# Attention heads with v stationary: probabilities scaled, turned by key block, output feature-major

## The chip, the cores and the metric

One core of one Trainium2 chip runs the whole program in one launch. TensorE (PE in the profile; PEld are its weight loads) multiplies, VectorE (DVE) and ScalarE (ACT) do elementwise work, GpSimd (POOL) a little of it, and SyncE's queue (SP) issues the transfers. The metric is the device time of one execution in microseconds; what is told of the kernel before is the median of its runs and one profiled execution.

## The reference

Three blocks follow one another on 512 tokens of 2048 features, all float32. Only the attention heads of the first and third block matter here.

```python
# block 1: 16 heads of 64, three dilated patterns mixed by their log-sum-exp
for window, dilation in ((128, 1), (512, 4), (2048, 16)):
    o, lse = dilated_pattern_attention(q, k, v, slopes, window, dilation)
weights = softmax(stack(lses), axis=0)
o = einsum('pbhs,pbhsd->bhsd', weights, stack(outs))
y_a = o * silu(g_a)

# block 3: 16 query heads on 4 key heads, blocks of 128, window 128, a sink per head
m = maximum(max(logits, axis=-1), sink)
p = exp(logits - m)
probs = p / (sum(p, axis=-1) + exp(sink - m))
out = einsum("bnhgqk,bnkhd->bnqhgd", probs, vb)
```

The kernel computes the first as one causal attention over 512 keys: the number of patterns that hold a key enters its bias as a logarithm, so that one softmax gives the mixture.

## The kernel before

Activations lie feature-major: 16 tiles of 128 features by 512 tokens. A **unit** is 128 output features of a projection: 16 feature tiles by 3 products (high and low halves of the split float32) into one PSUM bank of pool `pm`, 48 matmuls 128x512. They carry the names `pm<-a,wh` and `pm<-a,wl` and line L128 (the helper `mm`). A weight arrives by SP in pieces of 1024 columns; ScalarE makes its high half `wh` and VectorE its low half `wl`, into pools of five buffers each, ahead of the products.

Heads are generators. `drive` keeps 2 (block 1) or 5 (block 3) of them active; a head asks for a unit with `yield w, ct, h`, and each bare `yield` lets one step, 12 products of somebody's unit, be written in between. After every weight piece `bg` adds one step of background work: in blocks 1 and 2 the modulation products `ga<-gr` on VectorE (128x1024). A scheduler then sets the order on each engine from the dependencies; the four banks of pool `px` (tiles `x`) take everything that isn't a unit.

The dilated generator (`dilated`, eight pairs of heads in block 1, stretch 520 to 880 us) and the banded one (`swa`, eight pairs in block 3, mostly 2590 to 2960 us, one pair at a time) go alike. Per head and per block of 128 queries, scores of 128 to 512 keys are made (two matmuls), VectorE adds the bias and takes the extremum (L527, L1514), ScalarE exponentiates and sums (`den`). `turn` (L616) transposes the probabilities block by block of 128 keys with the identity `cst`, and ScalarE copies them out. `pv` then multiplies: the turned block 128x128 is stationary, 64 columns of v (`vt`, keys on partitions) move. The products of both heads lie in one bank with queries on the partitions; `finish_pair` divides by `den` on VectorE and transposes four blocks (L134, `tr4`) back to feature-major. `pipeline` writes scores, turn and product of neighbouring blocks one step apart, eight blocks for a dilated pair, four half-rows for a banded one.

The recurrence `hgrn` of block 1, which the prediction reads a row of, ends in a matmul `po[64 * r:64 * r + 64, c]` with a stationary of 64 columns: two chunks, one on each half of the output's partitions.

Of the kernel before, what the change touches and what calls it, by code (L numbers as in the profile page):

```python
# [14 lines left out]
AF = mybir.ActivationFunctionType  # L15
OP = mybir.AluOpType
AX = mybir.AxisListType.X

P = 128
T = 512  # L20
# [20 lines left out]
class Kernel:  # L41
# [524 lines left out]
    def dilated(self, p, h, w, ys):  # L566
        nc = self.nc
# [16 lines left out]
        self.act(vt, self.tr4(v))  # L584
        den = self.s(8)
        po = self.x()
        prs, pts = {}, {}

        def scores(i):
            qi, hh = i // 2, i % 2  # L590
            n = P * (qi + 1)
            sc = self.x()
            self.scores(sc[:, :n], q[hh][:, qi * P:(qi + 1) * P], [v[:, :n] for v in k[hh]])
            prs[i] = self.t()
            self.softmax_block(sc[:, :n], n, bts[hh][:, T - n:], den[:, i:i + 1], prs[i][:, :n])

        def turn(i):
            pts[i] = self.turn(prs.pop(i), i // 2 + 1)

        def out(i):  # L600
            qi, hh = i // 2, i % 2
            r = slice(64 * hh, 64 * hh + 64)
# [8 lines left out]

    def turn(self, pr, nb):

        b = self.x()
        for j in range(nb):
            self.nc.tensor.transpose(b[:, j * P:(j + 1) * P], pr[:, j * P:(j + 1) * P], self.ident)  # L616
        pt = self.t()
        self.act(pt[:, :nb * P], b[:, :nb * P])
# [8 lines left out]
    def finish_pair(self, po, den):  # L627

        rd = self.s(8)
        self.nc.vector.reciprocal(rd, den)  # L630
        on = self.t()
        self.tt(on.rearrange("p (n d) -> p n d", d=64), po.rearrange("p (n d) -> p n d", d=64),
                rd[:, :, None].to_broadcast([P, 8, 64]))
        yield
        ot = self.tr4(on)
        yo = self.y()
        self.act(yo, ot, scale=0.5)
        return yo

# [197 lines left out]
    def na(self, p, h, w, ys):  # L837
# [30 lines left out]
        yield  # L868
        vts = [self.turn(v, 4) for v in vs]
        den = self.s(8)  # L870
# [16 lines left out]
        def turn(j):  # L887
            pts[j] = self.turn(prs.pop(j), 4)

        def out(j):  # L890
            hh, half = j // 2, j % 2
            r = slice(64 * hh, 64 * hh + 64)
            pt = pts.pop(j)
            for i in range(2):
                cb = 2 * half + i
                self.pv(pt[:, 256 * i:256 * i + 256], vts[half], po[:, cb * P + 64 * hh:cb * P + 64 * hh + 64],
                        [(2 * i, r), (2 * i + 1, r)])

# [579 lines left out]
    def swa(self, i, h, w, kf, ys):  # L1478
# [18 lines left out]
        k, vt = kf[kv], self.vb[kv]  # L1497
        nm, den = self.s(8), self.s(8)
        po = self.x()
        prs, pts = {}, {}  # L1500

# [3 lines left out]

        def scores(j):
            hh, half = j // 2, j % 2
            hd = SWA_ORDER[2 * i + hh]
            sc, pr = self.x(), self.t()
            for qi, k0, c, n in blocks(half):  # L1510
                self.scores(sc[:, c:c + n], q[hh][:, qi * P:(qi + 1) * P], [a[:, k0 * P:k0 * P + n] for a in k[hh]])
            for qi, k0, c, n in blocks(half):
                m = nm[:, 2 * qi + hh:2 * qi + hh + 1]
                nc.vector.tensor_tensor_reduce(pr[:, c:c + n], sc[:, c:c + n], nbs[hh][:, 256 - n:256], 1.0,  # L1514
                                               self.nsink[:, hd:hd + 1], OP.add, OP.min, accum_out=m)
                self.act(pr[:, c:c + n], pr[:, c:c + n], AF.Exp, bias=m, scale=-1.0,
                         accum_out=den[:, 2 * qi + hh:2 * qi + hh + 1])
            prs[j] = pr

        def turn(j):  # L1520
            pts[j] = self.turn(prs.pop(j), 3 + j % 2)

        def out(j):
            hh, half = j // 2, j % 2
            r = slice(64 * hh, 64 * hh + 64)
            pt = pts.pop(j)
            for qi, k0, c, n in blocks(half):
                self.pv(pt[:, c:c + n], vt, po[:, qi * P + 64 * hh:qi * P + 64 * hh + 64],
                        [(k0 + b, r) for b in range(n // P)])

        yield from self.pipeline(4, scores, turn, out)
        es = self.s(8)
        for hh in range(2):
            hd = SWA_ORDER[2 * i + hh]
            self.act(es[:, hh::2], nm[:, hh::2], AF.Exp, bias=self.rowp[:, 16 + hd:17 + hd])
        self.tt(den, den, es, OP.add)
        ys[8 + i] = yield from self.finish_pair(po, den)

# [220 lines left out]
```

## Time and profile before

| | us |
|---|---|
| median of 3 runs (lowest, highest) | 3434.01 (3431.7, 3434.43) |
| profiled execution, its own time | 3428.47 |
| its span, first to last instruction | 3426.8 |
| TensorE busy | 3387.9 (99%) |
| VectorE busy | 1974.5 (58%) |
| ScalarE busy | 1277.3 (37%) |
| mean granted TensorE clock | 0.997 |

In a row of a group stand line, engine and operation, out<-in by the program's names, the shape (for matmuls ahead of it the stationary, partitions*columns), the number of instructions, then busy us, mean ns of one, and the idle time before them with what ended it. A row of the timeline begins with its start in us from the span's start and how long it was busy; like neighbours are merged (x8). A float32 matmul is two instructions, an fp32r one (units, scores) and a transposition are one.

### The profile page before, as it was taken

What the parts mean: (1) busy time and instruction counts of PE and PEld (TensorE: products, weight loads), DVE (VectorE), ACT (ScalarE), POOL (GpSimd) and SP (SyncE); (2) the same over time, 40 slices, a digit from 0 to 9 for tenths busy, and PEclk for the clock granted to TensorE, in tenths of its full rate; (3) what the DMA queues carried; (4) which work ended last, traced back from release to release, by engine and by line L of the source; (5) the groups of instructions that cost most, each with busy time, mean ns of one, the idle gap of its engine ahead of it and who ended that gap; (6) DMA issues with size and microseconds to landing.
All of it is one profiled execution on the core that took longest, in us unless ns stands there. A gap on an engine that the chain in (4) does not pass through costs nothing.

```text
span 3426.8 us, 44441 instructions
## 1 busy us (share of the span) xinstructions
PE 3387.9 (99%) x16688; PEld 2826.3 (82%) x16688; DVE 1974.5 (58%) x3593; ACT 1277.3 (37%) x2459; POOL 133.1 (4%) x156
## 2 busy tenths in 40 slices
PE   9999999999999999999999999999999999999999
PEld 7878888888888888888888888887888888888887
DVE  8677556556767555643367667666754333344552
ACT  4222244444334223544442243333334344432331
POOL 0000000000000000101100000000000000000000
PEclk9999999999999999999999999999999999999999
DMA  6355345435664445432234333322222233324442
GB/s 222 123 178 172 134 149 185 143 128 184 199 221 133 154 158 181 172 120 96 84 106 143 100 114 105 96 92 89 90 65 86 96 102 105 127 94 146 141 142 95
DMA packets 166168, 451.68 MB, mean 132 GB/s; under 512 B 26496, under 2 KB 47296, under 8 KB 165952
## 3 DMA queue, kind: packets, MB, share of 16 engines
q1 hardware_dynamic: 165952, 448.84, 39.8%
q8 instruction: 131, 2.15, 0.3%
q14 instruction: 85, 0.70, 0.1%
HBM read 423.58 MB, written 25.18 MB: 131 GB/s over the span
## 4 chain that ended last, share of the span: by engine, by line
PE 53%; DVE 4%; issue 1%; ACT 1%; POOL 0%; DMA 0%; SPq 0%; DVEq 0%; ACTq 0%; POOLq 0%
PE pm L128 46%; PE x L128 5%; DVE fp L117 1%; PE x L616 1%; PE x L134 1%; DVE wl L117 1%; DVE ft L1278 1%; DVE t L117 1%; DVE t L120 0%; ACT t L114 0%; POOL s L142 0%; ACT wh L114 0%; DVE s L1383 0%; DVE s L117 0%; DMA t<-in_w3s_dram 0%
## 5 line engine op out<-in xcount | busy, mean ns | idle before, releaser
L128 PE MATMUL pm<-a,wh 128*128 128x512 f32 x8512 | 2667.9, 394 | 5.4 <-ACT a L114 3.5
L128 PEld LDWEIGHTS pm<-a,wh 128*128 128x128 f32 x8512 | 1573.6, 188 | 319.4 <-ACT a L114 4.3
L128 PE MATMUL pm<-a,wl 128*128 128x512 f32 x4256 | 1666.0, 391 | 0.3 <-DVE wl L117 0.3
L114 ACT ACTIVATE wh<-wr 128x512 fp32r<-128x512 f32 (+2 forms) x1073 | 671.5, 627 | 1717.9 <-PE pm L128 1635.0
L117 DVE TENSOR_TENSOR wl<-wr,wh 128x512 fp32r<-128x512 f32 (+2 forms) x1073 | 740.1, 692 | 975.6 <-ACT wh L114 909.0
L128 PEld LDWEIGHTS pm<-a,wl 128*128 128x128 f32 x4256 | 801.0, 188 | 172.3 <-DVE wl L117 0.8
L120 DVE SCALAR_TENSOR_TENSOR ga<-gr,sc_c,ga 128x1024 f32<-128x1024 f32 x180 | 231.2, 1285 | 77.6 <-DMA gr<-in_wada_dram 77.4
L114 ACT ACTIVATE t<-x 128x512 f32<-128x512 f32 (+3 forms) x317 | 150.2, 488 | 105.0 <-PE x L128 47.0
L128 PEld LDWEIGHTS x<-t,t 128*128 128x128 f32 (+3 forms) x1296 | 156.2, 183 | 29.4 <-issue 8.7
L114 ACT ACTIVATE t<-t 128x512 f32<-128x512 f32 (+2 forms) x204 | 125.0, 613 | 142.8 <-DVE t L117 95.1
L128 PE MATMUL x<-t,t 128*128 128x64 f32 (+5 forms) x1296 | 168.0, 274 | 6.0 <-DVE t L117 6.0
L117 DVE TENSOR_TENSOR t<-t,t 128x512 f32<-128x512 f32 (+2 forms) x233 | 156.0, 670 | 22.0 <-ACT t L114 18.6
L114 ACT ACTIVATE t<-t,s 128x128 f32<-128x128 f32 (+2 forms) x192 | 98.5, 514 | 79.4 <-DVE s L527 60.3
L142 POOL TENSOR_TENSOR s<-s,nhalf 128x4 f32<-128x4 f32 (+1 forms) x51 | 60.7, 1191 | 1254.5 <-DVE s L125 1254.5
L616 PE MATMUL x<-cst,t 128*128 128x128 f32 x464 | 74.6, 275 | 4.1 <-ACT t L114 4.1
L134 PE MATMUL x<-cst,t 128*128 128x128 f32 x464 | 69.9, 273 | 6.5 <-DVE t L117 3.3
L134 PEld LDWEIGHTS x<-cst,t 128*128 128x128 f32 x464 | 56.2, 139 | 22.3 <-DVE t L117 3.0
L128 PE MATMUL x<-acc,t 128*128 128x128 f32 (+3 forms) x336 | 72.6, 310 | 0.0
L120 DVE SCALAR_TENSOR_TENSOR t<-t,pm 128x512 f32<-128x512 f32 x64 | 43.8, 684 | 46.2 <-PE pm L128 44.4
L114 ACT ACTIVATE t<-pm 128x512 f32<-128x512 f32 (+2 forms) x154 | 68.8, 482 | 0.2
L117 DVE TENSOR_TENSOR a<-t,a 128x512 fp32r<-128x512 f32 x96 | 63.7, 688 | 8.7 <-ACT a L114 8.5
L616 PEld LDWEIGHTS x<-cst,t 128*128 128x128 f32 x464 | 56.7, 152 | 9.4 <-ACT t L114 5.6
(230 smaller groups left out, 1652.5 us busy)
## 6 DMA issues: line engine op xcount, KB each, us to landing
wr<-in_w_dram SPq DMA_DIRECT2D x380, 512.0 KB, 3.3
gr<-in_wada_dram SPq DMA_DIRECT2D x192, 512.0 KB, 4.2
wr<-in_wo_dram SPq DMA_DIRECT2D x96, 512.0 KB, 3.4
t<-in_xt_dram SPq DMA_DIRECT2D x32, 256.0 KB, 3.6
res<-t SPq DMA_DIRECT2D x32, 256.0 KB, 2.0
t<-res SPq DMA_DIRECT2D x32, 256.0 KB, 2.8
gld<-t SPq DMA_DIRECT2D x32, 256.0 KB, 2.0
t<-gld SPq DMA_DIRECT2D x32, 256.0 KB, 2.7
```

The source lines that it names most:

```text
L114: return self.nc.scalar.activation(out, in_, fn, **kw)
L117: return self.nc.vector.tensor_tensor(out, a, b, op)
L120: return self.nc.vector.scalar_tensor_tensor(out, a, s, b, op0=op0, op1=op1)
L128: return self.nc.tensor.matmul(out, l, r, start=start, stop=stop, skip_group_check=True)
L134: self.nc.tensor.transpose(b[:, p * P:(p + 1) * P], src[:, p * P:(p + 1) * P], self.ident)
L142: self.nc.gpsimd.tensor_tensor(out, u, self.nhalf[:, :n], OP.pow)
L616: self.nc.tensor.transpose(b[:, j * P:(j + 1) * P], pr[:, j * P:(j + 1) * P], self.ident)
L1278: nc.vector.tensor_reduce(tv[:, :, i], pv, AX, OP.add, negate=True)
```

## The change

In both generators v becomes the stationary operand (64 columns of a block of 128 keys: one head's features) and the turned probabilities move. A product's output has one head's 64 features on half of the partitions and queries along the bank: it is feature-major as it comes, and `finish_pair` with its four transpositions falls away. Each block of probabilities is divided by its sum on VectorE before it is turned (`reciprocal`, then `ts`), since queries no longer lie on partitions afterwards. Turned blocks are gathered by key block: all queries that see key block j lie side by side and move in one matmul of 512, 384, 256 or 128 columns. So all scores of a pair come first, six steps with the widest first (four in the banded head), then the turns of both heads, then the products, two by two. In the banded head the sink's term is added before the reciprocal, per half-row. The neighbourhood heads of block 2 call `turn` in its new form and are otherwise as before.

```diff
-            self.softmax_block(sc[:, :n], n, bts[hh][:, T - n:], den[:, i:i + 1], prs[i][:, :n])
-            self.pv(pts.pop(i), vt, po[:, i * 64:i * 64 + 64], [(j, r) for j in range(qi + 1)])
-        yield from self.pipeline(8, scores, turn, out)
-        ys[8 + p] = yield from self.finish_pair(po, den)
+        a, b, c = [self.y() for _ in range(2)], [self.y() for _ in range(2)], self.y()
+        pr = lambda hh, qi: (b[hh][:, 384:512], c[:, 256 * hh:256 * hh + 256], b[hh][:, 0:384], a[hh])[qi]
+        def scores(hh, qs):
...
+            i, n = 4 * hh + qs[0], len(qs)
+            nc.vector.reciprocal(rd[:, i:i + n], den[:, i:i + n])
+            for qi in qs:
+                self.ts(pr(hh, qi), pr(hh, qi), rd[:, 4 * hh + qi:4 * hh + qi + 1])
+        def turn(hh, blocks):
+            return self.turn([pr(hh, qi)[:, j * P:(j + 1) * P] for j in blocks for qi in range(j, 4)])
+        for hh in range(2):
+            for qs in ((3,), (2,), (0, 1)):
+                scores(hh, qs)
+                yield
+        p0 = [turn(hh, (0,)) for hh in range(2)]
+        yield
+        po = self.x()
+        p13 = [turn(hh, (1, 3)) for hh in range(2)]
+        self.pv(po, vt, p0, 0, 0, T, True)
+        yield
+        p2 = [turn(hh, (2,)) for hh in range(2)]
+        self.pv(po, vt, p13, 1, P, 384)
+        self.pv(po, vt, [v[:, 384:] for v in p13], 3, 384, P)
+        yield
+        self.pv(po, vt, p2, 2, 256, 256)
+        yo = self.y()
+        self.act(yo, po, scale=0.5)
...
-    def pv(self, pt, vt, out, vs):
-        for j, (blk, c) in enumerate(vs):
-            self.mm(out, pt[:, j * P:(j + 1) * P], vt[:, blk * P + c.start:blk * P + c.stop],
-                    start=j == 0, stop=j == len(vs) - 1)
+    def pv(self, po, vt, pts, j, c, n, start=False):
+        for hh in range(2):
+            self.mm(po[64 * hh:64 * hh + 64, c:c + n], vt[:, j * P + 64 * hh:j * P + 64 * hh + 64], pts[hh][:, :n],
+                    start=start, stop=True)
...
+            o = slice(4 * hh + 2 * half, 4 * hh + 2 * half + 2)
+            self.act(es[:, o], nm[:, o], AF.Exp, bias=self.rowp[:, 16 + hd:17 + hd])
+            self.tt(es[:, o], es[:, o], den[:, o], OP.add)
+            nc.vector.reciprocal(es[:, o], es[:, o])
             for qi, k0, c, n in blocks(half):
+                self.ts(pr[:, c:c + n], pr[:, c:c + n], es[:, 4 * hh + qi:4 * hh + qi + 1])
...
+        t0 = [turn(hh, 0) for hh in range(2)]
+        yield
+        po = self.x()
+        t1 = [turn(hh, 1) for hh in range(2)]
+        self.pv(po, vt, t0, 0, 0, 256, True)
+        self.pv(po, vt, [v[:, 256:] for v in t0], 1, P, 256)
+        yield
+        self.pv(po, vt, t1, 2, 256, 256)
+        self.pv(po, vt, [v[:, 256:] for v in t1], 3, 384, P)
```

What this does to the order of the instructions is shown at two places on TensorE and one on VectorE. First TensorE in the first dilated pair of the kernel before, between two steps of unit products (`pm_3861`); `x_3760` is the pair's bank of products, `t_3752` is v, `t_3919` a block of turned probabilities, `x_3956` the next turned block, `x_3962` the next scores:

```order
L128 MATMUL pm_3861<-a_423,wl_3931 128x512
L128 MATMUL x_3760<-t_3752,t_3919 128x64 x3
L616 MATMUL x_3956<-cst,t_3924 128x128 x3
L128 MATMUL x_3962<-acc_522_3545,t_3353 128x512
L128 MATMUL x_3962<-acc_523_3546,t_3353 128x512
L128 MATMUL pm_3861<-a_449,wh_3934 128x512
```

And the same pair now, where the first products stand; the turns of key blocks 1 and 3 of both heads come ahead of them, and `t_3951` and `t_3958` are the turned rows of key block 0 of the two heads:

```order
L128 MATMUL pm_3861<-a_497,wl_3928 128x512
L638 MATMUL x_3973<-cst,t_3765 128x128
L638 MATMUL x_3973<-cst,t_3763 128x128
L638 MATMUL x_3973<-cst,t_3761 128x128 x2
L638 MATMUL x_3980<-cst,t_3765 128x128
L638 MATMUL x_3980<-cst,t_3764 128x128
L638 MATMUL x_3980<-cst,t_3762 128x128 x2
L128 MATMUL x_3972<-t_3951,t_3752 64x512
L128 MATMUL x_3972<-t_3958,t_3752 64x512
L128 MATMUL pm_4003<-a_155,wh_4006 128x512
```

Many products 64 columns wide became a few wide ones on 64 partitions, the second head's directly behind the first's, in all eight pairs of both kinds. Second, VectorE in the fifth dilated pair, at the last scores of the second head (L527 with `x_5670`; `t_5529` and `t_5530` are probabilities, `s_5525` the reciprocals, `wl` low halves of weights, `ga_5420` a modulation sum):

```order
L527 ISA t_5529,s_5675<-x_5670,t_5488 128x128
L527 ISA s_5675 128x1
L124 TENSOR_SCALAR t_5529<-t_5529,s_5525 128x384
L527 ISA t_5530,s_5678<-x_5670,t_5488 128x256
L527 ISA s_5678 128x1
L117 TENSOR_TENSOR wl_5819<-wr_5816,wh_5818 128x512
L120 SCALAR_TENSOR_TENSOR ga_5420<-gr_13_6151,sc_c_621,ga_5420 128x1024
L602 RECIPROCAL s_5525<-s_5524 128x2
L117 TENSOR_TENSOR wl_5823<-wr_5816,wh_5822 128x512
L124 TENSOR_SCALAR t_5529<-t_5529,s_5525 128x128
L124 TENSOR_SCALAR t_5530<-t_5530,s_5525 128x256
```

The scaling stands behind other work here; in the second, seventh and eighth pair it does so in like manner, in the other four the reciprocal and the multiplies follow the L527 rows directly.

Third, TensorE at the turns that take these blocks, from the last turn of the first head (`x_5709`) to those of the second (`x_5716`):

```order
L638 MATMUL x_5709<-cst,t_5526 128x128
L128 MATMUL pm_5624<-a_449,wh_5690 128x512
L128 MATMUL pm_5624<-a_450,wh_5690 128x512
L128 MATMUL pm_5624<-a_449,wl_5691 128x512
L128 MATMUL pm_5624<-a_475,wh_5690 128x512
L128 MATMUL pm_5624<-a_476,wh_5690 128x512
L638 MATMUL x_5716<-cst,t_5529 128x128
L638 MATMUL x_5716<-cst,t_5530 128x128
L638 MATMUL x_5716<-cst,t_5529 128x128
L638 MATMUL x_5716<-cst,t_5527 128x128
```

Five unit products were put between the two heads' turns; where the scaling isn't held up, the two heads' turns are neighbours.

More of the change, by code (lines that the diff above doesn't have):

```diff
@@ L868, in na @@
         yield
-        vts = [self.turn(v, 4) for v in vs]
+        four = lambda v: [v[:, i * P:(i + 1) * P] for i in range(4)]
+        vts = [self.turn(four(v)) for v in vs]
         den = self.s(8)
@@ L887, in turn @@
         def turn(j):
-            pts[j] = self.turn(prs.pop(j), 4)
+            pts[j] = self.turn(four(prs.pop(j)))
         def out(j):
@@ L895, in out @@
                 cb = 2 * half + i
-                self.pv(pt[:, 256 * i:256 * i + 256], vts[half], po[:, cb * P + 64 * hh:cb * P + 64 * hh + 64],
-                        [(2 * i, r), (2 * i + 1, r)])
+                for b in (0, 1):
+                    self.mm(po[:, cb * P + 64 * hh:cb * P + 64 * hh + 64], pt[:, 256 * i + b * P:256 * i + b * P + P],
+                            vts[half][:, (2 * i + b) * P + r.start:(2 * i + b) * P + r.stop], start=b == 0, stop=b == 1)
         yield from self.pipeline(4, scores, turn, out)
@@ L1518, in scores @@
[L1518 to L1526, printed above, removed]
-            for qi, k0, c, n in blocks(half):
[L1528 to L1532, printed above, removed]
@@ L1533, in swa @@
-        for hh in range(2):
[L1534 to L1537, printed above, removed]
+                                               self.nsink[:, hd:hd + 1], OP.add, OP.min, accum_out=nm[:, o:o + 1])
+                self.act(pr[:, c:c + n], pr[:, c:c + n], AF.Exp, bias=nm[:, o:o + 1], scale=-1.0,
+                         accum_out=den[:, o:o + 1])
@@ new lines, in scores, with turn @@
+                prs[hh, qi] = pr[:, c:c + n]
+            o = slice(4 * hh + 2 * half, 4 * hh + 2 * half + 2)
+            self.act(es[:, o], nm[:, o], AF.Exp, bias=self.rowp[:, 16 + hd:17 + hd])
+            self.tt(es[:, o], es[:, o], den[:, o], OP.add)
+            nc.vector.reciprocal(es[:, o], es[:, o])
+            for qi, k0, c, n in blocks(half):
+                self.ts(pr[:, c:c + n], pr[:, c:c + n], es[:, 4 * hh + qi:4 * hh + qi + 1])
+        def turn(hh, half):
+            if half == 0:
+                b = ((0, 0), (1, 0), (1, 1), (2, 0))
+            else:
+                b = ((2, 1), (3, 0), (3, 1))
+            return self.turn([prs[hh, qi][:, c * P:(c + 1) * P] for qi, c in b])
@@ new lines, in swa @@
+        for hh in range(2):
+            for half in range(2):
+                scores(hh, half)
+                yield
[5 more added lines that the diff above has]
+        self.pv(po, vt, [v[:, 256:] for v in t0], 1, P, 256)
+        yield
+        self.pv(po, vt, t1, 2, 256, 256)
+        self.pv(po, vt, [v[:, 256:] for v in t1], 3, 384, P)
+        yo = self.y()
```

61 lines of the change are left out of this document (24 added, 37 removed).

## The prediction

> **What bounds the kernel now.** I read the page first: busy shares, the rows by slice, the chain.
>
> ```profile
> span 3426.8 us, 44441 instructions
> PE 3387.9 (99%) x16688; PEld 2826.3 (82%) x16688; DVE 1974.5 (58%) x3593; ACT 1277.3 (37%) x2459; POOL 133.1 (4%) x156
> PE   9999999999999999999999999999999999999999
> L128 PE MATMUL pm<-a,wh 128*128 128x512 f32 x8512 | 2667.9, 394 | 5.4 <-ACT a L114 3.5
> ```
>
> TensorE has work in every slice. So two things only can move the time: how long TensorE streams, and where it has to stand. A busy time is no price here, since neighbouring matmuls overlap in the record (8512 x 394 ns would alone be 3354 us). I therefore price by starts: what an insert delays the next weight product. The windows of the two places that change, dilated (520 to 880 us) and banded (2650 to 2960 us), show full TensorE too, with VectorE at 61% and 36%:
>
> ```profile
> core 0: us, PE busy (x) PEld busy (x) DVE busy (x) ACT busy (x) POOL busy (x), PEclk, DMA share, GB/s
> 520.00:880.00 360.00, 356.68 (x1846) 302.16 (x1846) 220.11 (x379) 163.51 (x336) 0.00 (x0) 1.00 0.46 156
> 2650.00:2960.00 310.00, 310.00 (x1579) 262.45 (x1578) 112.45 (x248) 131.53 (x286) 9.82 (x6) 1.00 0.30 101
> ```
>
> **The old product.** From the timeline, a dilated insert (probabilities times v, then four turns), then a banded one (product alone):
>
> ```profile
> 647.29 1.00 PE L128 MATMUL x<-t,t 128*128 128x64 f32 x8
> 648.13 0.61 PE L616 MATMUL x<-cst,t 128*128 128x128 f32 x4
> 648.49 0.70 PE L128 MATMUL pm<-a,wh 128*128 128x512 f32 x2
> ...
> 2820.99 0.39 PE L128 MATMUL pm<-a,wl 128*128 128x512 f32 x1
> 2821.21 0.62 PE L128 MATMUL pm<-a,wh 128*128 128x512 f32 x2
> 2821.67 0.39 PE L128 MATMUL pm<-a,wl 128*128 128x512 f32 x1
> 2821.89 1.00 PE L128 MATMUL x<-vb,t 128*128 128x64 f32 x8
> 2822.70 0.71 PE L128 MATMUL pm<-a,wh 128*128 128x512 f32 x2
> ```
>
> Three weight products take 2821.67 - 2820.99 = 0.68 us, 0.227 each. An f32 matmul is two instructions (x8 is four 64-column blocks). Eight take 2822.70 - 2821.89 = 0.81 us, 0.101 each, however little they stream: what is paid is the load of a 128-column stationary. Four turns take 648.49 - 648.13 = 0.36. A dilated pair of heads has 20 blocks (40 instructions, 4.05 us) and the four turns of the finish (0.36): 4.41. A banded pair has 14 blocks (28 x 0.101 = 2.83) and the same finish: 3.19.
>
> **The new product.** No such matmul is in the trace, but its shape is: block 1's recurrence multiplies two halves of the output with a stationary of 64 columns each.
>
> ```profile
> 160.27 0.38 PE L128 MATMUL x<-t,acc 128*128 128x128 f32 x2
> 160.58 0.43 PE L128 MATMUL x<-t,t 128*64 128x128 f32 x2
> 160.94 0.49 PE L128 MATMUL x<-t,acc 128*128 128x128 f32 x2
> 161.36 0.44 PE L128 MATMUL x<-t,t 128*64 128x128 f32 x4
> 161.73 0.49 PE L128 MATMUL x<-t,acc 128*128 128x128 f32 x2
> ```
>
> One half alone (x2, the first chunk has no other) holds the queue 160.94 - 160.58 = 0.36 us, both halves (x4) 161.73 - 161.36 = 0.37. So the halves run at once. The price per column comes from the one wide f32 product, the per-feature mean:
>
> ```profile
> 878.16 0.39 PE L128 MATMUL pm<-a,wl 128*128 128x512 f32 x1
> 878.38 1.03 PE L128 MATMUL x<-t,ones 128*128 128x512 f32 x2
> 878.85 1.03 PE L128 MATMUL pm<-a,wh 128*128 128x512 f32 x2
> 879.72 0.39 PE L128 MATMUL pm<-a,wl 128*128 128x512 f32 x1
> ```
>
> From one wl product to the next lie 879.72 - 878.16 = 1.56 us; three weight products take 0.68 of it, so two passes of 512 columns cost 0.88, 1.72 ns per column. Going in and out of the half-width form costs too. The two passes of 128 columns are 0.22 of the 0.37, which leaves 0.15, and the full-width couple behind takes 0.42 (161.36 - 160.94) against 2 x 0.101: 0.22 more. That is 0.37 per group.
>
> A dilated pair moves 512 + 384 + 256 + 128 = 1280 columns per half in three groups: 1280 x 1.72 ns = 2.20, plus 3 x 0.37 = 1.11, in all 3.31. It saves 4.41 - 3.31 = 1.10, eight pairs 8.8 us. A banded pair moves 896 columns in two groups: 1.54 + 0.74 = 2.28, saves 0.91, eight pairs 7.3. The turns themselves (20 and 14) and the scores stay. Scores lose one small cost: behind turns they pay a late weight load. In the rows further down a set of four takes 2803.19 - 2802.73 = 0.46 us alone; a wider set of four behind turns takes 2806.73 - 2806.17 = 0.56. I give 0.08 of that 0.10 to the place, the rest to the width; some two to three places per pair go, 16 pairs: 3 us, and nothing as the lower end. **Sum on TensorE: 8.8 + 7.3 + 3 = 19 us.** Bounds: 16 without the last term; 25 if one entry price per pair (16 x 0.37 = 6) fell away where a group touches turns.
>
> By the Trainium skill, "TensorE: Matmul & The Clock Gate", section "Part 3: Packing small matmuls", matmuls start and end strictly in program order. The first half's second pass would then have to start before the second half's first, and a group would take three pass lengths, not two. Half as much stream again is 8 x 1.10 + 8 x 0.77 = 15 us, and the sum would be 4 instead of 19. The rows at 160.58 and 161.36 disagree (0.36 and 0.37, where a third pass of 128 columns would add 0.11), so I go by the rows.
>
> **What VectorE takes over.** Each probability block is now scaled before it is turned: 8 more multiplies per pair of heads, and the reciprocals come in small pieces. Prices:
>
> ```profile
> L120 DVE SCALAR_TENSOR_TENSOR ga<-gr,sc_c,ga 128x1024 f32<-128x1024 f32 x45 | 57.6, 1280 | 19.8 <-DMA gr<-in_wada_dram 19.7
> L124 DVE TENSOR_SCALAR ga<-gr,sc_c 128x1024 f32<-128x1024 f32 x3 | 2.2, 745 | 0.0
> L630 DVE RECIPROCAL s<-s 128x8 f32<-128x8 f32 x7 | 1.4, 203 | 0.2
> L117 DVE TENSOR_TENSOR t<-x,s 128x512 f32<-128x512 f32 x7 | 4.8, 685 | 0.0
> L114 ACT ACTIVATE s<-s,rowp 128x4 f32<-128x4 f32 x12 | 3.4, 283 | 0.0
> ```
>
> A multiply of n columns costs between 0.745 x n/1024 and that plus 0.2 (the reciprocal's fixed part). A dilated pair's 2560 columns in 8 pieces are 1.9 to 3.5 us, its six reciprocals at most 1.2, less 0.69 and 0.20 that go with the finish: 1 to 4 us, eight pairs 8 to 32 us in a stretch of 360 where VectorE has 140 free. It is hidden by weight products; the halves of a weight are made several products ahead. Without that cover the 8 to 32 us would be the price. In the banded stretch VectorE has 197 us free. ScalarE copies the same turned columns out, in six pieces instead of eight for a dilated pair; a banded pair has four small sink exponentials (0.28) instead of two. No transfer is added or moved on any queue.
>
> **The new wait.** The reciprocal stands on VectorE behind ScalarE's exponentials, and the turns of the second head wait for the scaled block. The trace has that chain up to the exponentials, for a set of 128 and 256 keys:
>
> ```profile
> 2802.73 0.62 PE L128 MATMUL x<-acc,t 128*128 128x128 f32 x4
> 2803.19 0.62 PE L128 MATMUL pm<-a,wh 128*128 128x512 f32 x2
> 2803.37 0.69 DVE L117 TENSOR_TENSOR wl<-wr,wh 128x512 fp32r<-128x512 f32 x1 [0.51 <-ACT wh L114]
> 2803.98 0.35 DVE L1514 CUSTOM_DVE_ANT_0 t<-x,t,nsink 128x128 f32<-128x128 f32 x1
> 2805.23 0.19 ACT L114 ACTIVATION_READ_ACCUMULATOR t<-t,s 128x1 f32 x1
> 2805.92 0.49 PE L616 MATMUL x<-cst,t 128*128 128x128 f32 x3
> 2806.17 0.72 PE L128 MATMUL x<-acc,t 128*128 128x256 f32 x4
> 2806.73 0.63 PE L128 MATMUL pm<-a,wh 128*128 128x512 f32 x2
> ```
>
> From the scores' start to the last exponential's sum are 2805.42 - 2802.73 = 2.69 us, with a weight's low half in VectorE's way. Reciprocal (0.20) and first multiply (0.2 to 0.3) make it 3.1 to 3.2. The changed order has one step of twelve weight products between, then the four turns of the first head: 0.46 + 12 x 0.227 + 0.36 = 3.5. So about 0.3 us to spare in the plain case. In a banded pair the sink's exponential and an add (0.28 and at most 0.20) come in between, but the late block is turned fourth, 0.3 later: as close. It isn't there where background work stands between reciprocal and multiply (the third excerpt of the order): a modulation step is 1.28 and can itself wait for its weights. What that does to a turn the old kernel shows:
>
> ```profile
> 568.65 1.28 DVE L120 SCALAR_TENSOR_TENSOR ga<-gr,sc_c,ga 128x1024 f32<-128x1024 f32 x1 [1.83 <-DMA gr<-in_wada_dram]
> 570.73 0.33 PE L616 MATMUL x<-cst,t 128*128 128x128 f32 x1 [1.56 <-ACT t L114]
> ...
> L616 PE MATMUL x<-cst,t 128*128 128x128 f32 x136 | 24.1, 277 | 3.3 <-ACT t L114 3.3
> ```
>
> TensorE stood 1.56 us, and before all turns of the dilated stretch 3.3 us (the group's row). In the changed order four of the eight dilated pairs have such work in between, and the turns of their second head stand behind up to five weight products more (1.1 us). Nothing at all is one end; 1.56 in all sixteen pairs, 25 us, the other. I take 1.5 for each of the four and next to nothing for the rest, 6 us, nearest to the row at 570.73. The old 3.3 go, since the small blocks are no longer turned one step behind their scores. Queued behind a waiting reciprocal are low halves of weights; they are made ahead, so nobody waits for them yet.
>
> **Sum:** -19 + 6 - 3 = -16 us. The profiled execution took 3428.47 us (span 3426.8 and 1.7 around it), so 3412 for it; the median of the runs shown is 5.5 longer, 3434.0, so **3418 us**. A measurement of this kernel tells about 0.2% (6.9 us) from no change.
>
> **The rivals.**
> - *The waits eat it.* Every pair stands about as at 570.73, or late low halves hold weight products: 16 x 1.4 = 22 us for the 6. That gives 3434, no change. For it: 0.3 us of margin, VectorE idle for its modulation weights. Against it: in the banded stretch no modulation runs, and turns are put later where work is in between. Chance 0.12.
> - *Three passes per group*, by the order rule above: 15 of the 19 go, 3433. Against it the two rows. Chance 0.04.
> - *The halves run one after the other* for moving widths of 256 to 512. The trace shows them at once for 128 columns only; two wide f32 streams may not both be fed. Each group then streams twice: 8 x 2.20 + 8 x 1.54 = 30 us more, 3448. It decides as soon as over half of the overlap is lost (16 of 30). Chance 0.08.
> - *No waits at all and dear entries shared*: 25 + 3 saved, 3406. Chance 0.10. That is the same mechanism and a larger size.
> - *The halves are torn apart* by the scheduler and nothing overlaps: the order shows each second half directly behind its first, so 0.01, with the time of the third rival.
>
> My forecast, 3410 to 3427, has the remaining 0.65. **Chances:** faster 0.65 + 0.10, and 0.03 of the first rival's low side, 0.78; within 0.2%, the rest of the first and the second, 0.13; slower 0.09. The range, 3406 to 3434, leaves out the serial halves (0.09), half of the case below it (0.05) and the worst of the waits (0.06).
>
> **What would show it.** Rows of form 128*64 128x512 in the timeline: four records and, to the next full-width start, about 1.2 us say right, 2.1 say serial, 1.7 three passes. The groups of form 128x64 by t, rows and vb lose 272 blocks, 544 instructions; those of L134 lose 64 turns. Idle time before the turns (L638) should be near 6 us and named ACT or DVE. VectorE's busy time rises 10 to 45 us with no idle time of pm products behind it. I am wrong if the L638 turns idle over 15 us, if pm products wait on wl, or if stalls move into the recurrence heads that run beside the first banded pair.

## The result and the profile after

The changed kernel took 3413.53 us (median of 4, 3408.87 to 3420.09), the kernel before, beside it on the same chip, 3432.86 (median of 4, 3431.28 to 3434.43). The ratio is 0.9939 with a 95% interval of 0.9925 to 0.9953, so 16 to 26 us less. A second measurement of the same kernel, among the experiments, gave 0.9935 (0.9917 to 0.9953). The forecast was 3418 us, 16 less.

From the page of the changed kernel come the span, the busy times, and the costliest group of weight products.

```profile
span 3412.6 us, 43830 instructions
PE 3370.2 (99%) x16336; PEld 2777.0 (81%) x16336; DVE 2010.0 (59%) x3793; ACT 1272.6 (37%) x2459; POOL 131.5 (4%) x156
L128 PE MATMUL pm<-a,wh 128*128 128x512 f32 x8512 | 2669.2, 394 | 6.2 <-ACT a L114 3.6
```

TensorE still bounds it at 99%. VectorE is busy 2010.0 - 1974.5 = 35.5 us longer, and nobody waits for that in the weight products: their idle time is 6.2 us against 5.4 before. Then the same two windows as before (dilated, banded; columns as in the prediction):

```profile
520.00:880.00 360.00, 356.16 (x1693) 282.64 (x1692) 236.40 (x458) 161.11 (x328) 0.00 (x0) 1.00 0.48 160
2650.00:2960.00 310.00, 310.00 (x1519) 253.09 (x1519) 128.68 (x341) 136.00 (x309) 9.83 (x6) 1.00 0.31 104
```

Both are as full as before on TensorE, with 16 us more on VectorE in each, and room left there. What changed its form shows in the groups by shape over the whole span; first the kernel before, then the changed one:

```profile
L128 PE MATMUL x<-t,t 128*128 128x64 f32 x576 | 74.4, 265 | 0.0
L134 PE MATMUL x<-cst,t 128*128 128x128 f32 x464 | 69.9, 273 | 6.5 <-DVE t L117 3.3 <-DVE t L120 2.0 <-POOL t L457 1.1
L128 PE MATMUL x<-rows,t 128*128 128x64 f32 x112 | 14.3, 268 | 0.0
L128 PE MATMUL x<-vb,t 128*128 128x64 f32 x112 | 14.2, 267 | 0.0
```

```profile
L134 PE MATMUL x<-cst,t 128*128 128x128 f32 x400 | 60.3, 273 | 6.1 <-DVE t L117 2.9 <-DVE t L120 2.1 <-POOL t L457 1.1
L128 PE MATMUL x<-t,t 128*128 128x64 f32 x256 | 31.9, 268 | 0.0
L128 PE MATMUL x<-t,t 128*64 128x512 f32 x32 | 8.6, 618 | 0.0
```

The narrow passes by t fall from 576 to 256, those by rows and vb (112 each) are gone: 544 instructions. The turns of the finish (L134) fall by 64. In their place stand few wide ones with 64 stationary columns (one of several such rows is shown).

**The new product, by starts.** TensorE's timeline of the changed kernel: start, length of the record, line, names, shape and count. A dilated pair's three groups, then a banded pair's second one:

```profile
530.53 0.39 PE L128 MATMUL pm<-a,wl 128*128 128x512 f32 x1
530.76 1.04 PE L638 MATMUL x<-cst,t 128*128 128x128 f32 x8
531.73 1.08 PE L128 MATMUL x<-t,t 128*64 128x512 f32 x4
532.74 0.73 PE L128 MATMUL pm<-a,wh 128*128 128x512 f32 x2
...
535.37 0.39 PE L128 MATMUL pm<-a,wl 128*128 128x512 f32 x1
535.61 0.60 PE L638 MATMUL x<-cst,t 128*128 128x128 f32 x4
536.13 1.08 PE L128 MATMUL x<-t,t 128*64 128x384 f32 x8
537.15 0.73 PE L128 MATMUL pm<-a,wh 128*128 128x512 f32 x2
...
539.78 0.39 PE L128 MATMUL pm<-a,wl 128*128 128x512 f32 x1
540.10 0.65 PE L128 MATMUL x<-t,t 128*64 128x256 f32 x4
540.68 0.73 PE L128 MATMUL pm<-a,wh 128*128 128x512 f32 x2
...
2813.99 0.39 PE L128 MATMUL pm<-a,wl 128*128 128x512 f32 x1
2814.31 0.87 PE L128 MATMUL x<-t,vb 128*64 128x256 f32 x8
2815.11 0.74 PE L128 MATMUL pm<-a,wh 128*128 128x512 f32 x2
```

(The row at 536.13 holds four records of 384 columns and four of 128; the one at 2814.31 four of 256 and four of 128.) Eight turns and the 512-column group delay the next weight product by 532.74 - 530.53 - 0.227 = 1.98 us. Eight turns alone cost 0.79 where they stand alone (530.22 to 531.01 in a row shown with the last experiment), so the group costs 1.19. The second one costs 537.15 - 535.37 - 0.227 - 0.36 = 1.19, the third 540.68 - 539.78 - 0.227 = 0.67. A dilated pair pays 3.05 us where 4.41 stood. In a banded pair the last group costs 2815.11 - 2813.99 - 0.227 = 0.89, and the two products of 256 columns before it 1.19 (1.77 with six turns that alone cost 0.58, from the timelines of this kernel and of the last experiment): 2.08 where 3.19 stood.

**Where the time went, by stage.** I divide each span at instructions that both kernels have: start to the first product of block 1's output stage (the dilated heads end there), block 3 with its output stage (from the end of block 2's side work), and all the rest, which no edit touches. In us, one profiled execution each, with all kernels of the experiments:

```
                     to end of    block 3 and    all the
                     dilated      its output     rest       span
before               878.4        1397.6         1150.8     3426.8
changed              869.2        1388.2         1155.3     3412.6
changed, again       867.5        1388.0         1150.8     3406.3
dilated heads only   868.2        1399.0         1153.4     3420.5
banded heads only    880.1        1388.1         1149.8     3418.0
torn halves          882.6        1388.2         1154.4     3425.2
head by head         864.4        1388.0         1152.3     3404.6
no scaling           866.4        1387.6         1155.3     3409.2
one step more        867.6        1388.2         1150.4     3406.2
mods left out        864.9        1387.8         1156.3     3409.0
scaling on ScalarE   869.5        1387.8         1153.8     3410.9
one group            861.0        1384.6         1155.2     3400.9
one group, again     864.1        1384.7         1149.7     3398.4
```

The dilated part gives 9.2 to 10.9 us, block 3 with its output 9.4 to 9.6. The rest moves by up to 6.6 us from one execution to the next for kernels that are identical there; the profiled execution of the changed kernel had 4.5 of that against it. So a difference of a few us between two spans says little, and the two first columns are what the experiments are read from (block 3 repeats within 0.6 us with the new heads and lies 1.4 apart in the two profiles with the old ones; the dilated part repeats within 2 to 3).

Most of that scatter has a name in the traces: TensorE's idle time, and stretches of 3.41 us at half the clock. In the changed kernel's profile the granted clock is 0.51 from 583.3 to 586.7 us, and weight products start 0.43 us apart there instead of 0.227, so one such stretch costs about 1.7 us. Take off the idle time and half of each such stretch, and the rest is 1138.2 to 1139.0 us in all thirteen profiles; the dilated part is 861.2 and 861.3 with the old dilated heads and 849.3 to 850.9 in the eight profiles with the new ones (torn halves and one group apart); block 3 is 1383.0 and 1383.4 with the old heads and 1372.5 to 1373.1 with the new ones.

**Where TensorE still stands.** The group of the probability turns between 465 and 872 us, then one of three places, in the fifth pair, all engines, with the weight products left out:

```profile
L638 PE MATMUL x<-cst,t 128*128 128x128 f32 x160 | 23.3, 275 | 3.8 <-DVE t L124 3.8
...
688.95 0.19 ACT L114 ACTIVATION_READ_ACCUMULATOR t<-t,s 128x1 f32 x1
689.02 1.28 DVE L120 SCALAR_TENSOR_TENSOR ga<-gr,sc_c,ga 128x1024 f32<-128x1024 f32 x1
...
690.21 0.16 DVE L602 RECIPROCAL s<-s 128x2 f32<-128x2 f32 x1
690.29 0.67 DVE L117 TENSOR_TENSOR wl<-wr,wh 128x512 fp32r<-128x512 f32 x1
690.88 0.54 DVE L124 TENSOR_SCALAR t<-t,s 128x128 f32<-128x128 f32 x2
...
691.21 0.81 PE L638 MATMUL x<-cst,t 128*128 128x128 f32 x4 [1.44 <-DVE t L124]
```

The last exponential's sum is there at 689.14; the reciprocal starts at 690.21, since a low half and a modulation step (ga) are ahead of it on VectorE, and another low half gets between it and the multiplies. TensorE stood 1.44 us. In the seventh pair (0.62 us) a modulation step stands ahead of the reciprocal in the same way. In both places that step began without idle time of VectorE before it (689.02 and 795.25), so it is its own 1.28 us that holds up the queue there, and not a wait for its weights. In the kernel before it was the other way: the steps ahead of the two stalls of 1.56 us began at 568.65 and 678.51, after waiting 1.83 and 1.71 us for their weights.

The longest of the three places, in the third pair, is of another kind:

```profile
581.13 0.17 DVE L602 RECIPROCAL s<-s 128x2 f32<-128x2 f32 x1 [0.71 <-ACT t L114]
...
581.67 0.59 PE L638 MATMUL x<-cst,t 128*128 128x128 f32 x2 [1.71 <-DVE t L124]
```

No modulation step is close: the last one began at 571.92. VectorE took up the last scores, there since 576.8, only at 579.79, behind the block before (with its reciprocal and multiply) and two low halves. The three places make 3.8 us, against 3.3 before. This number repeats badly: the same dilated code stood 4.1 us in a second profile and 2.2 in the profile of the dilated heads alone.

### The profile page after: what moved, and what is told of

Its sections match the earlier page's. It is cut to its first block, busy times and chain, and to the rows that moved or that the text cites. A ratio compares the mean times of both kernels' runs of the same rounds, so it can differ in the third digit from the quotient of the medians.

```text
span 3412.6 us, 43830 instructions
## 1 busy us (share of the span) xinstructions
PE 3370.2 (99%) x16336; PEld 2777.0 (81%) x16336; DVE 2010.0 (59%) x3793; ACT 1272.6 (37%) x2459; POOL 131.5 (4%) x156
## 4 chain that ended last, share of the span: by engine, by line
PE 86%; DVE 7%; DMA 3%; issue 2%; ACT 1%; POOL 0%; SPq 0%; DVEq 0%; ACTq 0%; POOLq 0%
PE pm L128 76%; PE x L128 8%; DMA gr<-in_wada_dram 3%; PE x L638 1%; DVE wl L117 1%; PE x L134 1%; DVE ga L120 1%; DVE t L117 1%; DVE fp L117 1%; DVE t L120 1%; DVE ft L1290 1%; ACT t L114 0%; ACT wh L114 0%; DMA t<-in_xt_dram 0%; DVE t L527 0%
## 5 line engine op out<-in xcount | busy, mean ns | idle before, releaser
L114 ACT ACTIVATE t<-x 128x512 f32<-128x512 f32 (+4 forms) x301 | 143.7, 505 | 83.1 <-PE x L128 50.7
L128 PE MATMUL x<-t,t 128*128 128x128 f32 (+8 forms) x1104 | 146.1, 295 | 7.5 <-DVE t L117 7.4
L128 PEld LDWEIGHTS x<-t,t 128*128 128x128 f32 (+3 forms) x1104 | 117.8, 175 | 33.7 <-issue 19.3
L114 ACT ACTIVATE t<-t,s 128x512 f32<-128x512 f32 (+2 forms) x192 | 98.5, 513 | 96.0 <-DVE s L527 63.0
L638 PE MATMUL x<-cst,t 128*128 128x128 f32 x464 | 66.7, 275 | 5.8 <-DVE t L124 3.8
L638 PEld LDWEIGHTS x<-cst,t 128*128 128x128 f32 x464 | 55.5, 144 | 17.1 <-DVE t L124 6.1
L128 PE MATMUL x<-acc,t 128*128 128x256 f32 (+3 forms) x336 | 66.4, 297 | 0.0
L134 PE MATMUL x<-cst,t 128*128 128x128 f32 x400 | 60.3, 273 | 6.1 <-DVE t L117 2.9
L134 PEld LDWEIGHTS x<-cst,t 128*128 128x128 f32 x400 | 48.3, 140 | 19.8 <-DVE t L120 2.9
```

The source lines that it names most:

```text
L114: return self.nc.scalar.activation(out, in_, fn, **kw)
L128: return self.nc.tensor.matmul(out, l, r, start=start, stop=stop, skip_group_check=True)
L134: self.nc.tensor.transpose(b[:, p * P:(p + 1) * P], src[:, p * P:(p + 1) * P], self.ident)
L638: self.nc.tensor.transpose(b[:, j * P:(j + 1) * P], src, self.ident)
```

## The experiments

The ratio in each is against the kernel before on the same chip, with its 95% interval. The lines of the diffs are against the changed kernel.

### Each half of the change alone

Dilated heads new and banded heads as before; then the other way round. The whole generators were exchanged, so the diffs stand here in outline:

```diff
-    def swa(...):        # new: key-block turns, v stationary
+    def swa(...):        # as before, with turn, pv and finish_pair as before
```
```diff
-    def dilated(...):    # new
+    def dilated(...):    # as before, with turn, pv and finish_pair as before
```

> The dilated heads in the new form, the banded heads as before. My theory (the gain is streaming time of TensorE, paid per pair of heads): of the 14 us by which the two profiled spans differ, the dilated stretch keeps its 9.4 us (first dilated scores to the first output tile), so 9 to 11 us faster than the kernel before. Rival (the gain comes mostly from what follows, block 3): under 4 us faster.

> The banded heads in the new form, the dilated heads as before. My theory: 8 to 11 us faster than the kernel before, and with the run of the dilated heads alone the two gains add up to the whole 19 us within 4 us. Rival (the two changes share something, say a stall that only both together remove): the two gains miss the whole by over 5 us.

Measured: dilated only 3421.94 us, ratio 0.9971 (0.996 to 0.9982); banded only 3421.4 us, 0.9971 (0.9959 to 0.9982); the kernel before 3431.89. Each half gives 10 us, and together they make up the whole. In the stage table each shows in its own column alone (868.2 and 1399.0; 880.1 and 1388.1). So there is no hidden exchange between the two places, and the stalls did not move into block 3's recurrence heads (from the start of block 3 on, TensorE is not busy for 17.9 us before and 17.2 after).

### Do the two halves of the output run at once?

If they do, the second head's product costs nothing as long as it is a neighbour of the first's. Torn halves: in the dilated pairs the second head's turns are put between the first and the second half's product, in two of three groups.

```diff
-        p13 = [turn(hh, (1, 3)) for hh in range(2)]
-        self.pv(po, vt, p0, 0, 0, T, True)
+        p13 = []
+        for hh in range(2):
+            p13.append(turn(hh, (1, 3)))
+            self.pv(po, vt, p0, 0, 0, T, True, (hh,))
...
+            self.pv(po, vt, p13, 1, P, 384, hhs=(hh,))
+            self.pv(po, vt, [v[:, 384:] for v in p13], 3, 384, P, hhs=(hh,))
```

> In the dilated heads the turns of the second head stand between the two halves of a product, for the groups of 512 and of 384 + 128 columns; nothing else differs from the changed kernel. If the halves overlap when they are neighbours, each torn group streams 0.88 us more and pays one entry of 0.37 more: 2 x 1.25 x 8 pairs = 20 us above the changed kernel, so about the time of the kernel before. If neighbouring halves don't overlap either, only the entries are added: 6 us above the changed kernel.

Measured: 3426.8 us, 0.9987 (0.9977 to 0.9997). TensorE's timeline of the torn kernel:

```profile
530.37 0.40 PE L128 MATMUL pm<-a,wl 128*128 128x512 f32 x1
530.61 0.60 PE L642 MATMUL x<-cst,t 128*128 128x128 f32 x4
531.13 1.07 PE L128 MATMUL x<-t,t 128*64 128x512 f32 x2
532.14 0.66 PE L642 MATMUL x<-cst,t 128*128 128x128 f32 x4
532.72 1.07 PE L128 MATMUL x<-t,t 128*64 128x512 f32 x2
533.73 0.73 PE L128 MATMUL pm<-a,wh 128*128 128x512 f32 x2
```

One half of 512 columns (x2) takes 532.14 - 531.13 = 1.01 us to the next start, exactly what both halves (x4) take in the changed kernel (532.74 - 531.73). The whole place costs 533.73 - 530.37 - 0.227 = 3.13 against 1.98: 1.15 more, and as much in the second group. Two groups in eight pairs make 18.4 us, where 20 was expected; the dilated part is 13 to 15 us longer than in the changed kernel and, with idle time and half clock taken off, 17 to 19 (868.4). That makes it slower than in the kernel before (882.6 against 878.4). So the overlap exists, and where two of three groups lose it nothing is left of the gain of the dilated heads.

Head by head: the halves stay neighbours, but where a group has two products, both of the first head are written first, then both of the second (in the banded heads alike).

```diff
-        self.pv(po, vt, p13, 1, P, 384)
-        self.pv(po, vt, [v[:, 384:] for v in p13], 3, 384, P)
+        for hh in range(2):
+            self.pv(po, vt, p13, 1, P, 384, hhs=(hh,))
+            self.pv(po, vt, [v[:, 384:] for v in p13], 3, 384, P, hhs=(hh,))
```

> Where a group has two products per head (384 + 128 in the dilated heads, 256 + 256 and 256 + 128 in the banded ones), the first head's two are written first, then the second head's two. If TensorE takes the next matmul of a free half wherever it stands in the queue, nothing changes: within 3 us of the changed kernel, a group of 512 columns still 0.88 us plus entry. If it keeps to the written order, the halves overlap by one pass at most: 0.43 to 0.88 us more per group of 512 and 0.4 to 0.65 per group of 384, which is 10 to 19 us over 24 groups.

Measured: 3411.26 us, 0.9945 (0.9925 to 0.9965). The second group there:

```profile
533.23 0.39 PE L128 MATMUL pm<-a,wl 128*128 128x512 f32 x1
533.46 0.60 PE L639 MATMUL x<-cst,t 128*128 128x128 f32 x4
533.99 1.09 PE L128 MATMUL x<-t,t 128*64 128x384 f32 x8
535.01 0.73 PE L128 MATMUL pm<-a,wh 128*128 128x512 f32 x2
```

It costs 535.01 - 533.23 - 0.227 = 1.55, as in the changed kernel. Now four passes of the first head (384, 384, 128, 128 columns) are in the queue ahead of the second head's first. The single records behind the row at 533.99 begin at 533.987 and 534.001, then at 534.361 and 534.374, both pairs with 384 columns: the two heads run side by side. (Two passes of one head by itself begin 0.48 us apart, at 531.135 and 531.616 in the torn kernel; and the record at 534.001 is the one that waits for the second head's turned rows.) So the second head's first pass began 0.36 us ahead of the first head's second, which stands ahead of it in the queue.

### What the turns wait for

The changed kernel was run again beside three edits. Its expectation and result:

> The changed kernel itself, as the mark for the three others: 3409 to 3420 us, 0.6% below the kernel before.

3411.16 us, ratio 0.9935 (0.9917 to 0.9953), turns idle 4.1 us between 465 and 872 us.

No scaling: the reciprocals and multiplies of the probability blocks are left out, in the banded heads too (the output lacks the division).

```diff
-            nc.vector.reciprocal(rd[:, i:i + n], den[:, i:i + n])
-            for qi in qs:
-                self.ts(pr(hh, qi), pr(hh, qi), rd[:, 4 * hh + qi:4 * hh + qi + 1])
```

> Reciprocals and multiplies are left out in both kinds of heads, so the probabilities are turned and multiplied undivided and the attention output lacks its division; all else is the changed kernel. My theory: the scaling costs only the standing of TensorE before the dilated turns, 3.8 us in the profile of the changed kernel, and nothing in the banded heads: 3 to 5 us faster than the changed kernel, the banded stretch the same to 1 us. Rival (VectorE's 35 us of added work also slows what lies around, through late halves of weights): over 8 us faster.

Measured: 3413.58 us, 0.9942 (0.9927 to 0.9958). The 3 to 5 us did not come: 866.4 in the dilated part against 867.5 and 869.2. The group of the turns, then VectorE, ScalarE and TensorE at the worst place:

```profile
L634 PE MATMUL x<-cst,t 128*128 128x128 f32 x160 | 22.3, 274 | 2.3 <-ACT t L114 2.3
...
684.78 1.28 DVE L120 SCALAR_TENSOR_TENSOR ga<-gr,sc_c,ga 128x1024 f32<-128x1024 f32 x1
685.97 0.29 DVE L527 CUSTOM_DVE_ANT_0 t<-x,t 128x128 f32<-128x128 f32 x1
...
686.30 0.40 ACT L114 ACTIVATE t<-t,s 128x128 f32<-128x128 f32 x1 [1.38 <-DVE s L527]
...
686.85 0.33 PE L634 MATMUL x<-cst,t 128*128 128x128 f32 x1 [1.77 <-ACT t L114]
```

Here, in the fifth pair, the turn waits for the exponential itself without the scaling, that for the bias and maximum on VectorE (L527), and that for ga. So the scaling was only the last member of a chain that is late anyway; my theory of this run, that reciprocal and multiply are the cause, fell. The turns stand 2.3 us in all. That is less than the 3.8 and 4.1 of the changed kernel, but not less than the 2.2 of the dilated heads alone, which do scale, so the run doesn't show that the scaling costs anything. The new theory was ga.

One step more: a further step of the schedule between the last scores and the first turn of each pair, in both kinds of heads.

```diff
+        yield
         p0 = [turn(hh, (0,)) for hh in range(2)]
```

> One bare yield more between the last scores and the first turns in both kinds of heads, twelve more unit products for the chain of exponential, reciprocal and multiply. If that chain is what TensorE stands for, the turns' idle time falls from about 4 us to under 1 and the kernel is 3 to 4 us faster than the changed one. If a longer pair only moves the standing elsewhere (tiles held longer, the next pair later), no gain.

Measured: 3406.39 us, 0.9921 (0.9906 to 0.9935). The median is 5 us below that of the changed kernel beside it, but the intervals overlap, the stages that were edited don't show it (867.6 and 1388.2), and one turn still stands 2.34 us, until 690.65; two modulation steps (687.79 and 689.11) are ahead of its multiply. Idle time under 1 us was expected, and it is 2.3. I take the gain for unclear.

Modulation left out while dilated heads run: its steps there issue no transfer and no multiply-add (later modulations lack these terms). `hold` is set while a dilated head is under way.

```diff
             for k in range(KT):
+                if k and self.hold:
+                    yield
+                    continue
                 raw = self.gp.tile([P, 1024], F32, name=f"gr{self.n}_{k}", tag="gr", bufs=2)
                 nc.sync.dma_start(raw, wada[sl, k])
```

> The changed kernel, but while any dilated head is under way the modulation's background steps do nothing: their weight transfers and their multiply-adds on VectorE (ga) are left out, so later modulations lack most of their terms. Theory (the turns of the dilated stretch stand because a ga step, waiting for its weights, is ahead of the scaling on VectorE): idle time ahead of the turns falls from 3.8-4.1 us to under 1, the dilated stretch from 403.0-403.5 us to 399-400.5, the median 3 to 4 us below that of the changed kernel (ratio to before about 0.9925). Rival (the turns stand because VectorE is full with low halves of weights and the attention's own blocks, whatever runs in the background): idle 3 us or more, stretch 402.5-403.5.

Measured: 3408.04 us, 0.9925 (0.9907 to 0.9943). The groups of ga and of the turns between 465 and 872 us:

```profile
L120 DVE SCALAR_TENSOR_TENSOR ga<-gr,sc_c,ga 128x1024 f32<-128x1024 f32 x23 | 29.5, 1282 | 8.5 <-DMA gr<-in_wada_dram 8.3
L642 PE MATMUL x<-cst,t 128*128 128x128 f32 x160 | 22.5, 274 | 0.1
```

With 23 of 45 ga steps left there, the idle time ahead of the turns is 0.1 us. The dilated part takes 864.9, 13.5 less than in the kernel before: about 8 x 1.28 = 10.2 from the inserts and the 3.3 that the turns stood there before. (By the stretch that the expectation names it is 397.1 against 403.0 and 403.5, where 399 to 400.5 was expected; but that stretch began 2 to 3 us later, which is why I read the sum from the start.) So without the modulation steps no turn stands, scaling or not. This run takes their transfers away too; that it is their 1.28 us and not their wait for weights is read from the profile of the changed kernel, for the fifth and the seventh pair. How a step that began nearly 10 us earlier makes the third pair stand, by the queue on VectorE that it leaves behind, is argued and not shown.

Scaling on ScalarE: the 128 multiplies, of both kinds of heads, as activations with a scale.

```diff
-                self.ts(pr(hh, qi), pr(hh, qi), rd[:, 4 * hh + qi:4 * hh + qi + 1])
+                self.act(pr(hh, qi), pr(hh, qi), scale=rd[:, 4 * hh + qi:4 * hh + qi + 1])
```

> The changed kernel with the multiplies of the probability blocks on ScalarE instead of VectorE (128 of them, 0.25 to 0.6 us each; the reciprocals stay on VectorE). If the place behind ga on VectorE is what the turns wait for: only the reciprocal is still behind it, so the idle time stays near 4 us (3 to 5), since the reciprocal has the same queue ahead; ratio 0.9935 as the changed kernel. Rival (VectorE's sheer load of 35 us more is what counts): idle falls under 2 us, stretch under 402. VectorE's busy time falls by 25 to 45 us in both cases.

Measured: 3415.05 us, 0.9949 (0.993 to 0.9968). VectorE's busy time falls to 1975.3, and the turns stand longer (their group between 465 and 872 us):

```profile
L638 PE MATMUL x<-cst,t 128*128 128x128 f32 x160 | 23.6, 279 | 5.6 <-ACT t L114 5.5
```

5.6 us is above the 3 to 5 expected, and not under the 2 that would have spoken for VectorE's sheer load. The reciprocal keeps its place behind ga: at the worst place (3.69 us, until 690.02) two modulation steps, at 685.84 and 688.18, stand ahead of it on VectorE. The multiply on ScalarE follows at once there (689.57, the reciprocal having begun at 689.38).

### One group per pair

Since a group's entry has a price, all turns of a pair come first and all its products stand in one group (in the banded heads alike).

```diff
-        po = self.x()
         p13 = [turn(hh, (1, 3)) for hh in range(2)]
-        self.pv(po, vt, p0, 0, 0, T, True)
         yield
         p2 = [turn(hh, (2,)) for hh in range(2)]
+        yield
+        po = self.x()
+        self.pv(po, vt, p0, 0, 0, T, True)
         self.pv(po, vt, p13, 1, P, 384)
         self.pv(po, vt, [v[:, 384:] for v in p13], 3, 384, P)
-        yield
         self.pv(po, vt, p2, 2, 256, 256)
```

> All turns of a pair first, then all its products in one group, so that a dilated pair goes into the half-width form once instead of three times, a banded pair once instead of twice. In the changed kernel's inserts an entry costs 0.33 us where turns stand ahead and 0.25 where unit products do: two entries less, 0.66 us per dilated pair, and one less, 0.33, per banded pair: 8 us faster than the changed kernel, 3405. Rival (the price is not per group but lies in each product, or the longer held tiles make others wait): under 3 us.

> The version with all turns of a pair first and all its products in one group, a second time, beside the two others: ratio 0.9914 again (0.990 to 0.993), dilated stretch 395 to 397 us, block 3 with its output stage near 1384.6. If the first result was partly a lucky place of stalls elsewhere, 0.9925 with the same stretch times there.

Measured: 3403.08 us, 0.9914 (0.9897 to 0.9931), and again 3402.96 us, 0.9917 (0.9897 to 0.9937). TensorE's timeline:

```profile
530.22 1.03 PE L638 MATMUL x<-cst,t 128*128 128x128 f32 x8
531.01 0.71 PE L128 MATMUL pm<-a,wh 128*128 128x512 f32 x2
...
536.83 0.39 PE L128 MATMUL pm<-a,wl 128*128 128x512 f32 x1
537.15 2.37 PE L128 MATMUL x<-t,t 128*64 128x512 f32 x16
539.45 0.73 PE L128 MATMUL pm<-a,wh 128*128 128x512 f32 x2
```

All 1280 columns cost 539.45 - 536.83 - 0.227 = 2.39 us where three groups cost 3.05. Eight dilated pairs give 8 x 0.66 = 5.3; eight banded ones 8 x 0.33 = 2.6 (1.75 against 2.08, from the same kernel's timeline). Block 3 with its output shows 3.3 to 3.6 less (1384.6 and 1384.7), the dilated part 3.4 to 8.2 less: its stretch took 395.2 and then 398.7, where 395 to 397 was expected the second time. The second profile has the turns standing 2.6 us and a turn of the projections 1.7 (0.8 in the second profile of the changed kernel). It is faster than the kernel before. Against the changed kernel the intervals of the ratios overlap a little (0.9931 and 0.9937 against 0.9917 at their near ends); what speaks for a gain is block 3, which repeats within 0.6 us, and the starts.

## Why the prediction was right, step by step

**TensorE's 19 us.** The price per column held: between weight products a group of 256 columns costs 0.67 us and one of 1280 costs 2.39, so 1.68 ns per column, where 1.72 was forecast. The price of going in and out was too high: 0.37 a group was taken from a couple of narrow full-width products behind the halves; measured are 1.19 - 0.88 = 0.31 next to turns and 0.67 - 0.44 = 0.23 between weight products. So the products save 1.36 in a dilated pair (1.10 forecast) and 1.11 in a banded one (0.91), 19.8 us over both instead of 16.1. The 3 us for scores that no longer stand behind turns hardly came. In the banded pair around 2803 all inserts together, by starts, cost 6.57 before and 5.31 after, so 1.26 - 1.11 = 0.15 is left for the scores; in the dilated pairs, with the turns now in odd places, 9.39 and 8.11 on average: 1.28 saved, 0.08 less than the products give. Over all that is 8 x 0.15 - 8 x 0.08 = 0.6 us, not 3.

**The new wait, 6 us.** Measured 3.8 and 4.1, and 2.2 with the dilated heads alone. The mechanism was right only in part. Of the four pairs with background work in between (second, fifth, seventh, eighth) two stood, 1.44 and 0.62 us, and the other two didn't. The third pair, taken for a plain one with 0.3 us to spare, stood longest, 1.71. And it isn't reciprocal and multiply that make a turn late: the run without them still stands 1.77 us at the worst place, and the run without ga 0.1 in all. That three places come to 3.8 us, not far from 6, is largely luck. **The old 3.3 us** were said to go because small blocks are no longer turned one step behind their scores. What showed is an exchange: 3.3 went and 2.2 to 4.1 came. Modulation steps are in it before and after, but before it was their wait for weights and now it is their length. 10.2 us by starts (8 x 1.28), with between 1.1 more and 0.8 less for the exchange, make 9.4 to 11.3 in the dilated part, where the table has 9.2, 10.2 and 10.9.

**The sum.** Forecast 16, measured 19.3 by the medians beside each other (16 to 26 by the interval). With the measured terms it is 19.8 + 0.6, with 0.8 less to 1.1 more for the exchange: 19.6 to 21.5. Three terms were mis-sized: the entry price (3.7 too little saved), the scores (2.4 too much) and the exchange of waits (at most 0.8 where I had 6 - 3 = 3). That the first two nearly cancel is luck; the 3 us by which the forecast fell short are about the wait's. In block 3 by itself 8 x 1.26 = 10.1 stands against 9.4 to 9.6 in the table, and against 9.9 to 10.9 with idle time and half clock taken off.

**VectorE's 10 to 45 us, hidden.** 35.5 came. A multiply of 512 columns cost 0.48 us, a reciprocal 0.16; the two groups of reciprocals between 520 and 880 us:

```profile
L602 DVE RECIPROCAL s<-s 128x1 f32<-128x1 f32 x25 | 4.0, 160 | 4.3 <-ACT t L114 4.3
L602 DVE RECIPROCAL s<-s 128x2 f32<-128x2 f32 x13 | 2.1, 161 | 4.3 <-ACT t L114 4.3
```

The last column shows the reciprocals waiting for ScalarE's exponentials, 8.6 us in that stretch, with VectorE idle and low halves queued behind. Weight products waited 0.5 us for low halves in the whole span, against 0.3 before. Taking the 35 us away (scaling on ScalarE) gained nothing.

**The rivals.** Serial halves, the one that would have made it slower, is ruled out by the wide rows: 1.01 us for one half of 512 columns and for two. The torn kernel shows what it would have cost. Three passes per group, by the order rule in the Trainium skill, "TensorE: Matmul & The Clock Gate", section "Part 3: Packing small matmuls", did not happen. The run head by head speaks against the rule for stationaries in different columns: a pass that is fifth in the queue began with the first, and the group cost the same 1.55 us. The waits that eat the gain did not come beyond what they had been before. Of the rival that went further (no waits, entries shared, 3406) the first half did not happen; the one-group version shares the entries by its layout and took 3403.

**What stays open.** What sets the idle time and the half-clock stretches that move the untouched rest from profile to profile; whether one more step before the turns is worth anything; and which part of VectorE's queue makes the third pair stand.

## What to carry to other kernels

With a stationary of 128 columns an instruction cost 0.101 us here with 64 columns moving, no less than a turn with 128 (0.36 for four). So where few columns move, turn the product round: make the small operand (here v, 64 columns) stationary and let the long one move, two heads side by side, and put the halves of both directly next to each other. Then make the groups few: each group had an entry of 0.2 to 0.3 us, and one group per pair instead of two or three gave another 6 to 9 us by the medians (ratios 0.9914 and 0.9917 against 0.9935 and 0.9939), 8 by the starts. Where an engine's queue holds long background work (here steps of 1.28 us), look for it ahead of the operation on which TensorE waits, before blaming the operation itself: taking the scaling away gained nothing, and taking the background away ended the stalls.

## What was not expected of the hardware

The order in which the halves' products are written makes no difference: two half-width products with stationaries in different columns begin 14 ns apart (533.987 and 534.001) even with three more passes of the first head between them in the queue. A half alone costs as much as both, for 128 columns (0.36 and 0.37 in the kernel before) and for 512 (1.01 and 1.01). And the price of a change between full and half width depends on the neighbour, 0.23 us between weight products and 0.31 next to turns.

A stall can cost more than its length. Between 465 and 872 us six of the thirteen profiles have a stretch of 3.41 us at a granted clock of 0.5, and each began within 1.7 us of the end of a stall of 1.7 us or more (in the changed kernel at 583.3, behind the stall that ended at 581.67). Four stalls of that length had none behind them.
